# Clearing transfers one by one from the SP queue, and unread products of ones at four places, in a one-core transformer kernel

## The chip, the cores and the metric

The kernel runs on one core of one Trainium2 chip. The metric is device time in microseconds (us) of one execution, lower is better. TensorE (PE) multiplies, PEld loads its weights, VectorE (DVE), ScalarE (ACT) and GpSimd (POOL) do the elementwise work, and the queues of SP, ACT and POOL issue transfers (DMA).

## The reference

The input is one sequence of 512 tokens with 1024 features. The first block is differential attention and a mixture of 16 experts; the second has two layers (an even and an odd mixer, each followed by a gated feed-forward) and a last normalisation. The part around the change, cut to what matters:

```python
x = x + diff_attention(rmsnorm(x, norm_mix), ...)        # 8 heads, two softmaxes each
x = x + hier_moe(rmsnorm(x, norm_ffn), ...)              # 4 groups x 4 experts, 2 experts per token
for layer in range(2):
    h = h + (even_mixer if layer == 0 else odd_mixer)(rms_norm(h, ...), ...)
    h = h + conv_gated_ffn(rms_norm(h, ...), ...)
return rms_norm(h, norm_out_g)
```

In the expert part a token goes to the two best experts of its best group. Each expert has a gate and an up matrix (1024 x 512 each) and a down matrix (512 x 1024).

## The kernel before, in words

Activations lie with features on the 128 partitions (`h`, 8 chunks of 128 x 512). Every fp32 product is made from three matmuls: weights and activations are split into a rounded half and the rest (`wh`, `wl`; `xh`, `xl`), and `mm3` (L129 on, its matmuls are L135 to L141) adds three of the four cross products. ScalarE rounds the weights (`wh`, L110) and VectorE subtracts (`wl`, L111), so each stretch of matmuls needs both halves first.

The stages stand in the order of `run`: a (attention), b (experts), c (even mixer), d (feed-forward), e (odd mixer), f (feed-forward), z (last norm). `emit` runs a list of units of work, each with a cost in us, and `after(us, fn)` puts off a piece of work until units of that cost have gone by. A scheduler then orders the instructions of each engine before the run, so instructions that don't depend on each other can stand in another order than in the code. On the chip each engine takes its list strictly in order, and a waiting instruction holds all behind it.

Stage a. `project` makes q, k and v of four heads at a time. `headnorm` normalises q and k: ScalarE scales (`qs`, L449) and squares, VectorE sums and runs a reciprocal square root of 12 small steps (`rsq`, L286 to L293), VectorE scales (L466), TensorE transposes four 128 x 128 pieces (`t`, L472) into the one PSUM bank of that kind, and ScalarE copies them out (`kt`, two copies, L477). The next transposes wait for these copies. The first weights are split in four pieces of one chunk, as they land. `norm_r` takes the sums of squares through TensorE (`ss`, L349), then the same chain of small steps (`rt`).

After the first q and k, `moe_begin` loads constants, and `zero_rows` (L1254) clears the table `yb` in HBM, 1024 rows of 1024, to which the experts later scatter their results: one tile of zeros `zr`, 16 transfers of 256 KB, all issued by ScalarE's queue.

`route` (from L1298) makes the choice of experts: VectorE works out the logits and masks, TensorE counts ranks (`rk`, L1334) and finds the token numbers of the first two experts (`tk`, L1410), and POOL gathers the tokens' rows from HBM (`xe`, L1451). Stage b then starts: `weigh` (L1363) makes the weights `w` on VectorE and splits them on POOL into `tokv` (L1397), `places` picks them per expert (`tkb`, L1410), and `prep` transposes the gathered rows (L1462) and splits them (`xeh`, `xel`). `gate_up`, `act` and `down` run 16 experts. The last loop (L1600 on) adds the results into `h` and starts the next norm chunk by chunk; stage c begins with products of 290 columns.

`self.onesr` is a 128 x 128 tile of ones, `ptt` takes a PSUM bank of kind `t` (one in stage a, two in stage b).

Of the kernel before, what the change touches and what calls it, by code (L numbers as in the profile page):

```python
# [4 lines left out]
F32 = mybir.dt.float32  # L5
# [9 lines left out]
T, D, P = 512, 1024, 128  # L15
NT, NK = T // P, D // P
# [65 lines left out]
class K:  # L82
# [314 lines left out]
    def stage_a(self):  # L397
# [4 lines left out]
        with tc.tile_pool(name="pa", bufs=1) as pa:  # L402
# [6 lines left out]
            self.small_loads()  # L409
            dist = pa.tile([P, T], F32, name="c_dist")  # L410
            nc.sync.dma_start(dist, a["cst"][:, _CST["dist"][0]:_CST["dist"][0] + T])

            lv = pa.tile([P, 2, 64], F32, name="lv", tag="wk", bufs=6)
            ls = pa.tile([P, 2], F32, name="ls")
# [838 lines left out]

    def zero_rows(self, pool):  # L1254

        z = pool.tile([P, T], F32, name="zr", tag="wk", bufs=6)
        self.nc.gpsimd.memset(z, 0.0)
        for i in range(2 * NT):
            for c in range(2):
                self.nc.scalar.dma_start(self.yb[i * P:(i + 1) * P, c * T:(c + 1) * T], z)  # L1260

    def route_step(self, pool):

# [32 lines left out]
    def route(self):  # L1296
# [31 lines left out]
        Mb = pr.tile([P, NT, NE], BF, name="Mb")  # L1328
        nc.vector.tensor_tensor(Mb, f1, f2, op=OP.add)

        rk = self.pst("rk")
        for i in range(NT):
            for j in range(i + 1):
                nc.tensor.matmul(rk[:, i * NE:(i + 1) * NE], lhsT=self.onesb if j < i else self.before, rhs=Mb[:, j],  # L1334
                                 start=j == 0, stop=j == i, skip_group_check=True)
# [86 lines left out]
    def stage_b(self):  # L1422
# [5 lines left out]
        with tc.tile_pool(name="pb", bufs=1) as pb:  # L1428
# [20 lines left out]
            def gather(e):  # L1449
                xe = xes[e % 3]  # L1450
                nc.gpsimd.indirect_dma_start(out=xe, out_offset=None, in_=xn[:, :], bounds_check=T - 1, oob_is_err=False,  # L1451
                                             in_offset=bass.IndirectOffsetOnAxis(ap=self.gix[:, e:e + 1], axis=0))

            def prep(e):
                xe = xes[e % 3]
                xh = pb.tile([P, NK, P], F32R, name="xeh", tag="xeh", bufs=2)
                xl = pb.tile([P, NK, P], F32R, name="xel", tag="xel", bufs=2)
                for hf in range(2):
                    tp = self.ptt()
                    for q in range(4):  # L1460
                        kk = hf * 4 + q
                        nc.tensor.transpose(tp[:, q * P:(q + 1) * P], xe[:, kk * P:(kk + 1) * P], self.ident)  # L1462
                    sl = slice(hf * 4, hf * 4 + 4)
                    tv = tp.rearrange("p (a b) -> p a b", a=4)
                    nc.scalar.copy(xh[:, sl], tv)  # L1465
                    nc.vector.tensor_tensor(xl[:, sl], tv, xh[:, sl].bitcast(F32), op=OP.subtract)
                return xh, xl

            def gate_up(e, x):
                ps = []  # L1470
                for src in (wg[e], wu[e]):
                    acc = self.mmt()
                    sv = src.rearrange("(k p) n -> p k n", p=P)
                    for k0 in (0, 4):
                        raw = load(sv[:, k0:k0 + 4], 4, 512)
                        for c in (0, 2):
                            h, l = split(raw[:, c:c + 2], [P, 2, 512])
                            for k in (0, 1):
                                q = k0 + c + k
                                self.mm3(acc, h[:, k], l[:, k], x[0][:, q], x[1][:, q], q == 0, q == NK - 1, swap=True)  # L1480
                    ps.append(acc)
                return ps
# [63 lines left out]
            def spread(acc, e, y, m):  # L1546
                for n in range(2):
                    nc.tensor.matmul(acc, lhsT=y[n][:, m * P:(m + 1) * P], rhs=ohw[e], start=n == 0 and e == NE - 2, stop=False,
                                     skip_group_check=True)
# [12 lines left out]
            gather(0)  # L1562
            gather(1)
            self.weigh()
            tk = self.pvt("tkb")
            for e in range(2):
                self.places(e, tk, 6, 9)
            xs = {0: prep(0)}
            ps = gate_up(0, xs.pop(0))
            for e in range(2, 4):  # L1570
                self.places(e, tk, 0, 9)
# [2 lines left out]
            for e in range(NE - 2):  # L1574
# [5 lines left out]
                ps = gate_up(e + 1, xs.pop(e + 1))  # L1580
# [8 lines left out]
            ps = gate_up(NE - 1, xs.pop(NE - 1))  # L1589
# [9 lines left out]
            for m in range(NK):  # L1599
                acc = self.mmt()  # L1600
                spread(acc, NE - 2, yo, m)
                spread(acc, NE - 1, ye, m)
                for i in range(NT):
                    nc.tensor.matmul(acc[:, i * P:(i + 1) * P], lhsT=ys[i][1][:, m * P:(m + 1) * P], rhs=self.ident,
                                     start=False, stop=i == NT - 1, skip_group_check=True)
                self.last_add(m, acc)

    def overflow(self, pb):

# [224 lines left out]
```

## Time and profile before

| | |
|---|---|
| median of 3 runs | 1873.79 us (1873.08 to 1877.85) |
| the profiled execution | 1876.64 us, its span 1874.9 us |
| mean granted TensorE clock | 0.984 of full |
| PE, DVE, ACT, POOL busy | 97%, 69%, 54%, 12% of the span |
| HBM read, written | 238.19 MB, 15.73 MB |

The profile shows one execution. A busy PE need not be a fast one: a matmul of 512 columns starts every 0.23 us at the full clock and every 0.43 at the half clock, and the shares don't tell these apart. What ends the waits of each stretch, and how closely matmuls follow one another there, is read from the timelines.

### The profile page before, as it was taken

The numbers are of one execution on the slowest core, as the hardware profiler recorded it, in microseconds if no ns is written. First come the engines' busy times: TensorE is split into PE (matmuls) and PEld (weight loads), VectorE is DVE, ScalarE is ACT, GpSimd is POOL, SyncE is SP. The second block draws the span as 40 slices with busy tenths as digits, with TensorE's granted clock in tenths as the row PEclk, the third lists the DMA queues.
The fourth block names the chain that finished last, engine by engine and source line by source line (L and its number), as shares of the span: only waits on it lengthen the run. The fifth ranks groups of instructions, "written<-read, shape, count | busy, mean of one in ns | idle before, by whom it ended". The sixth has DMA issues, their size and how long they took to land.

```text
span 1874.9 us, 24863 instructions
## 1 busy us (share of the span) xinstructions
PE 1810.7 (97%) x8700; PEld 1464.2 (78%) x8701; DVE 1291.1 (69%) x2571; ACT 1019.8 (54%) x1787; POOL 222.5 (12%) x277
## 2 busy tenths in 40 slices
PE   8899997999998899999999999999999999999997
PEld 6688885778887787777888888888776788888885
DVE  6477857999997789755777357734567677537753
ACT  5467756888885347666544234433467544324442
POOL 2000012222222211320200000012100200000001
PEclk9899998999999899999999999999999999999998
DMA  5654657999995356562332333234544233243321
GB/s 193 206 136 116 177 166 267 353 370 368 371 368 188 108 138 167 135 164 74 107 98 69 104 108 106 69 97 135 145 127 108 75 91 100 77 121 91 91 85 61
DMA packets 278196, 287.36 MB, mean 153 GB/s; under 512 B 16150, under 2 KB 188598, under 8 KB 278064
## 3 DMA queue, kind: packets, MB, share of 16 engines
q1 hardware_dynamic: 268784, 270.15, 47.8%
q0 software_dynamic: 5072, 10.00, 1.5%
q10 hardware_dynamic: 4208, 5.56, 0.8%
q8 instruction: 70, 1.15, 0.3%
q14 instruction: 62, 0.51, 0.1%
HBM read 238.19 MB, written 15.73 MB: 135 GB/s over the span
## 4 chain that ended last, share of the span: by engine, by line
PE 59%; DVE 4%; DMA 1%; issue 1%; ACT 1%; POOL 1%; SPq 1%; DVEq 0%; POOLq 0%; ACTq 0%
PE mm L135 16%; PE mm L137 16%; PE mm L136 16%; PE pv L798 3%; PE s L765 2%; PE t L786 1%; DVE wl L111 1%; PE mm L140 1%; PE mm L139 1%; PE mm L141 1%; PE pv L1200 1%; DVE sc L964 1%; SPq L391 1%; DVE m L963 0%; DMA rsw<-qd 0%
## 5 line engine op out<-in xcount | busy, mean ns | idle before, releaser
L110 ACT CAST wh<-wr 128x1024 fp32r<-128x1024 f32 (+3 forms) x331 | 305.9, 925 | 361.9 <-PE mm L136 259.4
L111 DVE TENSOR_TENSOR wl<-wr,wh 128x1024 fp32r<-128x1024 f32 (+5 forms) x328 | 355.3, 1087 | 190.9 <-ACT wh L110 186.2
L135 PE MATMUL mm<-xh,wh 128*128 128x512 f32 x952 | 375.3, 394 | 2.1 <-DVE h L384 1.7
L137 PE MATMUL mm<-xh,wl 128*128 128x512 f32 x952 | 372.5, 391 | 0.0
L136 PE MATMUL mm<-xl,wh 128*128 128x512 f32 x952 | 371.9, 391 | 0.0
L135 PEld LDWEIGHTS mm<-xh,wh 128*128 128x128 f32 x952 | 179.2, 188 | 40.9 <-issue 4.2
L137 PEld LDWEIGHTS mm<-xh,wl 128*128 128x128 f32 x952 | 179.2, 188 | 38.2 <-issue 0.9
L136 PEld LDWEIGHTS mm<-xl,wh 128*128 128x128 f32 x952 | 179.3, 188 | 35.7
L111 DVE TENSOR_TENSOR wl<-wx,wh 128x1024 fp32r<-128x1024 f32 x123 | 151.9, 1251 | 13.0 <-ACT wh L110 6.8
L110 ACT CAST wh<-wx 128x1024 fp32r<-128x1024 f32 x134 | 139.5, 1050 | 25.2 <-PE mm L141 24.2
L139 PE MATMUL mm<-wh,xh 128*128 128x512 f32 (+3 forms) x384 | 138.1, 364 | 9.7 <-ACT wh L110 5.6
L140 PE MATMUL mm<-wl,xh 128*128 128x512 f32 (+3 forms) x384 | 137.5, 358 | 3.4 <-DVE wl L111 3.4
L137 PE MATMUL mm<-hh,wl 128*128 128x512 f32 x352 | 137.2, 390 | 0.0
L136 PE MATMUL mm<-hl,wh 128*128 128x512 f32 x352 | 137.1, 390 | 0.0
L135 PE MATMUL mm<-hh,wh 128*128 128x512 f32 x352 | 137.1, 389 | 0.0
L141 PE MATMUL mm<-wh,xl 128*128 128x512 f32 (+3 forms) x384 | 136.5, 356 | 0.0
L686 DVE TENSOR_TENSOR z<-mm,rb 128x512 f32<-128x512 f32 x88 | 60.3, 688 | 81.3 <-PE mm L137 81.3
L277 POOL TENSOR_TENSOR acc<-acc,sq 128x512 f32<-128x512 f32 x42 | 57.0, 1357 | 415.6 <-ACT sq L273 415.1
L139 PE MATMUL mm<-wh,xeh 128*128 128x512 f32 x256 | 103.6, 405 | 0.8 <-ACT xeh L1465 0.8
L140 PE MATMUL mm<-wl,xeh 128*128 128x512 f32 x256 | 101.6, 397 | 0.0
L141 PE MATMUL mm<-wh,xel 128*128 128x512 f32 x256 | 101.5, 396 | 0.0
L384 DVE TENSOR_TENSOR h<-mm,h 128x512 f32<-128x512 f32 x88 | 60.5, 689 | 47.1 <-PE mm L137 46.4
(414 smaller groups left out, 3394.9 us busy)
## 6 DMA issues: line engine op xcount, KB each, us to landing
wr<-in_ffn_w_up SPq DMA_DIRECT2D x88, 512.0 KB, 5.0
wx<-in_moe_w_gate SPq DMA_DIRECT2D x23, 1024.0 KB, 9.5
wx<-in_moe_w_up SPq DMA_DIRECT2D x22, 1024.0 KB, 8.9
wx<-in_moe_w_down SPq DMA_DIRECT2D x22, 1024.0 KB, 10.7
wr<-in_ffn_w_down SPq DMA_DIRECT2D x32, 704.0 KB, 4.7
kh<-nh SPq DMA_DIRECT2D x84, 128.0 KB, 2.3
wr<-in_moe_w_up SPq DMA_DIRECT2D x10, 1024.0 KB, 8.8
wr<-in_moe_w_down SPq DMA_DIRECT2D x10, 1024.0 KB, 11.3
```

What stands on the lines that cost most here:

```text
L110: nc.scalar.copy(h, raw)
L111: (nc.gpsimd if eng else nc.vector).tensor_tensor(l, raw, h.bitcast(F32), op=OP.subtract)
L135: mm(out, lhsT=wh, rhs=xh, start=first, stop=False, skip_group_check=True)
L136: mm(out, lhsT=wh, rhs=xl, start=False, stop=False, skip_group_check=True)
L137: mm(out, lhsT=wl, rhs=xh, start=False, stop=last, skip_group_check=True)
L139: mm(out, lhsT=xh, rhs=wh, start=first, stop=False, skip_group_check=True)
L140: mm(out, lhsT=xh, rhs=wl, start=False, stop=False, skip_group_check=True)
L141: mm(out, lhsT=xl, rhs=wh, start=False, stop=last, skip_group_check=True)
L277: nc.gpsimd.tensor_tensor(self.acc, self.acc, sq, op=OP.add)
L384: self.nc.vector.tensor_tensor(self.h[:, m], ps, self.h[:, m], op=OP.add)
L686: nc.vector.tensor_tensor(z[:, 2:], ps, self.rb, op=OP.mult)
L798: nc.tensor.matmul(pv[64 * e:64 * e + 64, j * P:], lhsT=heads[u]["v"](j), rhs=pt[:, 4 * j:3 * j + 4], start=j == 0, stop=j == NT - 1, skip ...
```

## The change

`zero_rows` makes the zeros in a tile of their own of 128 x 128, and issues 8 transfers of 512 KB (each partition's 512 bytes go out eight times) from SP instead of 16 of 256 KB from ScalarE, put off by 5, 11, ... 47 us of units. A new function `warm(n)` puts n matmuls of ones by ones (512 columns) into a bank of kind `t` that nobody reads; it is called at the start of stage a (6), before the rank counts of `route` (14), at the start of stage b (18) and after the last loop of stage b (8). In stage b `prep(0)` now stands ahead of the `places` of the first two experts.

```diff
--- before.py
+++ after.py
@@ -409,6 +409,7 @@
             self.small_loads()
             dist = pa.tile([P, T], F32, name="c_dist")
             nc.sync.dma_start(dist, a["cst"][:, _CST["dist"][0]:_CST["dist"][0] + T])
+            self.warm(6)
 
             lv = pa.tile([P, 2, 64], F32, name="lv", tag="wk", bufs=6)
             ls = pa.tile([P, 2], F32, name="ls")
@@ -1253,11 +1254,17 @@
 
     def zero_rows(self, pool):
 
-        z = pool.tile([P, T], F32, name="zr", tag="wk", bufs=6)
+        z = pool.tile([P, 128], F32, name="zr")
         self.nc.gpsimd.memset(z, 0.0)
         for i in range(2 * NT):
-            for c in range(2):
-                self.nc.scalar.dma_start(self.yb[i * P:(i + 1) * P, c * T:(c + 1) * T], z)
+            self.after(5 + 6 * i, lambda i=i: self.nc.sync.dma_start(
+                self.yb[i * P:(i + 1) * P].rearrange("p (c d) -> p c d", c=8), z[:, None, :].to_broadcast([P, 8, P])))
+
+    def warm(self, n):
+
+        ps = self.ptt("warm")
+        for _ in range(n):
+            self.nc.tensor.matmul(ps, lhsT=self.onesr, rhs=self.onesr[:, None, :].to_broadcast([P, NT, P]), start=True, stop=True)
 
     def route_step(self, pool):
 
@@ -1328,6 +1335,7 @@
         Mb = pr.tile([P, NT, NE], BF, name="Mb")
         nc.vector.tensor_tensor(Mb, f1, f2, op=OP.add)
 
+        self.warm(14)
         rk = self.pst("rk")
         for i in range(NT):
             for j in range(i + 1):
@@ -1562,10 +1570,11 @@
             gather(0)
             gather(1)
             self.weigh()
+            self.warm(18)
+            xs = {0: prep(0)}
             tk = self.pvt("tkb")
             for e in range(2):
                 self.places(e, tk, 6, 9)
-            xs = {0: prep(0)}
             ps = gate_up(0, xs.pop(0))
             for e in range(2, 4):
                 self.places(e, tk, 0, 9)
@@ -1604,6 +1613,7 @@
                     nc.tensor.matmul(acc[:, i * P:(i + 1) * P], lhsT=ys[i][1][:, m * P:(m + 1) * P], rhs=self.ident,
                                      start=False, stop=i == NT - 1, skip_group_check=True)
                 self.last_add(m, acc)
+            self.warm(8)
 
     def overflow(self, pb):
```

The changed lines move all numbers below them, by 1 after the first call, by up to 10 at the end. Three places of the engines' lists matter below.

ScalarE after the first q and k, before (`yb<-zr` are the clearing transfers, `kt` the copies out of the transposes' bank):

```order
L1246 DMA cr<-in_cst 128x388
L451 ACTIVATE sq<-qs 128x512
L1260 DMA yb<-zr 128x512 x16
L477 ACTIVATE kt<-t,vecs 128x2x128 x2
L110 CAST wh<-wr 128x1024 x2
L477 ACTIVATE kt<-t,vecs 128x2x128 x6
L716 CAST nh<-kt 128x512
L110 CAST wh<-wr 128x1024
```

and now:

```order
L1247 DMA cr<-in_cst 128x388
L452 ACTIVATE sq<-qs 128x512
L110 CAST wh<-wr 128x1024
L478 ACTIVATE kt<-t,vecs 128x2x128 x2
L110 CAST wh<-wr 128x1024
L478 ACTIVATE kt<-t,vecs 128x2x128 x6
L717 CAST nh<-kt 128x512
L110 CAST wh<-wr 128x1024
```

The 16 transfers are gone from the list, and one weight cast stands in their place. On SP the eight transfers now stand around the fifth of the first large weight loads; before it was

```order
L1717 DMA ident<-in_cst 128x128
L411 DMA c_dist<-in_cst 128x512
L128 DMA wr<-in_da_w_in 128x4x512 x5
L729 DMA qs<-nh 64x512
L730 DMA qs<-nl 64x512
```

and now

```order
L411 DMA c_dist<-in_cst 128x512
L128 DMA wr<-in_da_w_in 128x4x512 x4
L1260 DMA yb<-zr 1024x1x128 x5
L128 DMA wr<-in_da_w_in 128x4x512
L1260 DMA yb<-zr 1024x1x128 x3
L730 DMA qs<-nh 64x512
L731 DMA qs<-nl 64x512
```

VectorE at the end of the first four weight pieces, where the sums of squares `ss` come back from TensorE and `rtv` (L286) reads them; before:

```order
L311 SCALAR_TENSOR_TENSOR xl_110<-h,vecs,xh_108 128x512
L286 TENSOR_SCALAR rtv<-ss 128x4
L111 TENSOR_TENSOR wl<-wr,wh 128x1024
L287 TENSOR_SCALAR rty<-rtv 128x4
L111 TENSOR_TENSOR wl<-wr,wh 128x1024
L288 TENSOR_SCALAR rty<-rty 128x4
L291 TENSOR_TENSOR rtt<-rty 128x4
L292 SCALAR_TENSOR_TENSOR rtt<-rtt,rtv 128x4
```

and now:

```order
L287 TENSOR_SCALAR rty<-rtv 128x4
L288 TENSOR_SCALAR rty<-rty 128x4
L291 TENSOR_TENSOR rtt<-rty 128x4
L292 SCALAR_TENSOR_TENSOR rtt<-rtt,rtv 128x4
L293 SCALAR_TENSOR_TENSOR rt<-rtt,rty 128x4
L291 TENSOR_TENSOR rtt<-rt 128x4
L292 SCALAR_TENSOR_TENSOR rtt<-rtt,rtv 128x4
L293 SCALAR_TENSOR_TENSOR rt<-rtt,rt 128x4
L291 TENSOR_TENSOR rtt<-rt 128x4
L292 SCALAR_TENSOR_TENSOR rtt<-rtt,rtv 128x4
L293 SCALAR_TENSOR_TENSOR rt<-rtt,rt 128x4
L111 TENSOR_TENSOR wl<-wr,wh 128x1024 x3
```

The split of the next weights (`wl`, 128x1024) stood right behind the first small step, and stands now behind the whole chain; `rtv` is the row just ahead of the second list.

TensorE where the experts begin (`oh` are one-hot tiles, loaded as weights); before:

```order
L1410 MATMUL tk<-tokv,oh 128x6
L1462 MATMUL t<-ident,xe_3196 128x128 x8
L139 MATMUL mm<-wh,xeh 128x512
L140 MATMUL mm<-wl,xeh 128x512
L141 MATMUL mm<-wh,xel 128x512
L139 MATMUL mm<-wh,xeh 128x512
L140 MATMUL mm<-wl,xeh 128x512
L141 MATMUL mm<-wh,xel 128x512
L1410 LDWEIGHTS oh
L1410 MATMUL tkb<-tokv,oh 128x3
```

and now:

```order
L1418 MATMUL tk<-tokv,oh 128x6
L1267 MATMUL warm<-onesr 128x512 x18
L1470 MATMUL t<-ident,xe_3210 128x128 x8
L1418 LDWEIGHTS oh
L1418 MATMUL tkb<-tokv,oh 128x3
```

Three more `tkb` products follow, and then the expert products. The 18 products of ones stand ahead of the transposes of `prep(0)`, and the four `tkb` products, which read POOL's `tokv`, ahead of the first six expert products instead of behind them. On VectorE the last sum of `weigh` (`w`, L1388) stood behind the first `xel` of `prep(0)`, and stands now ahead of it. At the end of stage b the 8 products of the last call were parted: four stand behind the transposes of `hg` of the last expert, four behind the last loop.

## Rows read from the trace of the kernel before

**Rows 1.** The page, busy time: us, share of the span, instructions.
```profile
PE 1810.7 (97%) x8700; PEld 1464.2 (78%) x8701; DVE 1291.1 (69%) x2571; ACT 1019.8 (54%) x1787; POOL 222.5 (12%) x277
```

**Rows 2.** Timeline of ScalarE, 54 to 82 us: start, duration, instruction, [idle before, releaser].
```profile
61.26 10.38 ACTq L1260 DMA_DIRECT2D yb<-zr  x16
71.68 0.84 ACT L477 ACTIVATE kt<-t,vecs 128x256 f32<-128x256 f32 x2 [9.80 <-DMA yb<-zr]
```

**Rows 3.** Timeline of TensorE, 50 to 105 us; starts lie closer than durations, work overlaps.
```profile
61.46 0.39 PE L141 MATMUL mm<-wh,xl 128*128 128x512 f32 x1
...
64.41 0.60 PE L472 MATMUL t<-ident,qs 128*128 128x128 f32 x4
64.77 0.48 PE L139 MATMUL mm<-wh,xh 128*128 128x512 f32 x1
...
72.57 1.11 PE L472 MATMUL t<-ident,qs 128*128 128x128 f32 x4 [6.17 <-ACT kt L477]
...
79.53 0.60 PE L472 MATMUL t<-ident,qs 128*128 128x128 f32 x4
...
84.98 0.22 PE L526 MATMUL s<-kh,qs 128*128 128x128 f32 x1
```

**Rows 4.** Stretches: length, PE, PEld, DVE, ACT, POOL busy (count), PEclk, DMA share, GB/s.
```profile
5.60:10.40 4.80, 4.77 (x11) 3.46 (x12) 4.31 (x4) 4.41 (x8) 3.62 (x4) 1.00 1.04 391
...
30.00:40.00 10.00, 10.00 (x45) 8.26 (x45) 6.77 (x19) 7.12 (x10) 0.00 (x0) 1.00 0.01 3
...
280.00:281.00 1.00, 0.00 (x0) 0.00 (x0) 0.83 (x6) 0.58 (x1) 0.00 (x0) 0.62 1.05 403
```

**Rows 5.** Timeline of TensorE, 255 to 330 us.
```profile
279.32 0.64 PE L1288 MATMUL t<-ident,hg 128*128 128x128 f32 x4
285.00 0.17 PE L1334 MATMUL rk<-Mb,before 128*128 128x16 bf16 x1 [5.04 <-DVE Mb L1329]
...
293.35 1.94 PE L1462 MATMUL t<-ident,xe 128*128 128x128 f32 x8 [5.58 <-DMA xe<-xn,gix]
...
298.44 0.24 PE L1410 MATMUL tkb<-tokv,oh 128*128 128x3 bf16 x4 [0.67 <-POOL tokv L1397]
```

**Rows 6.** Timeline of TensorE, 574 to 665 us.
```profile
619.31 0.58 PE L139 MATMUL mm<-wh,xh 128*128 128x290 f32 x1 [3.18 <-DVE h L384]
...
625.28 0.30 PE L140 MATMUL mm<-wl,xh 128*128 128x290 f32 x1
...
627.42 0.30 PE L141 MATMUL mm<-wh,xl 128*128 128x290 f32 x1
```

**Rows 7.** Timeline of VectorE, 56 to 92 us.
```profile
67.28 1.29 DVE L466 TENSOR_TENSOR qs<-qs,rsq 128x512 f32<-128x512 f32 x2
```

**Rows 8.** Timeline of VectorE, 16 to 30 us.
```profile
22.95 1.23 DVE L111 TENSOR_TENSOR wl<-wr,wh 128x1024 fp32r<-128x1024 f32 x1
...
25.49 0.16 DVE L291 TENSOR_TENSOR rtt<-rty 128x4 f32<-128x4 f32 x1
...
27.06 0.16 DVE L293 SCALAR_TENSOR_TENSOR rt<-rtt,rt 128x4 f32<-128x4 f32 x1
```

**Rows 9.** Timeline of the SP queue, 0 to 120 us.
```profile
25.41 0.37 SPq L128 DMA_DIRECT2D wr<-in_da_w_in  x1
...
48.27 0.54 SPq L729 DMA_DIRECT2D qs<-nh  x1
```

**Rows 10.** The page, DMA issues: count, KB each, median us to landing.
```profile
wr<-in_ffn_w_up SPq DMA_DIRECT2D x88, 512.0 KB, 5.0
```

**Rows 11.** Timeline of TensorE, 20 to 33 us.
```profile
24.23 0.79 PE L140 MATMUL mm<-wl,xh 128*128 128x512 f32 x1 [0.35 <-DVE wl L111]
```

**Rows 12.** Timelines of ScalarE, VectorE and GpSimd, 276 to 312 us.
```profile
280.00 0.59 ACT L1290 COPY xk<-t 128x512 f32<-128x512 f32 x1 [1.20 <-PE t L1288]
...
295.09 0.69 DVE L1466 TENSOR_TENSOR xel<-t,xeh 128x512 fp32r<-128x512 f32 x1 [2.47 <-ACT xeh L1465]
...
295.98 0.47 POOL L1397 CAST tokv<-w 128x64 bf16<-128x64 f32 x1 [4.50 <-DVE w L1388]
```

## The prediction

> **What bounds the kernel now.** The page's busy times come first: TensorE has work in 97% of the span [rows 1], so a change counts by the gaps it closes in TensorE's row and by how fast the matmuls follow one another. I then looked for stretches with a gap and a low granted clock, and in each asked what ended the wait. Four matter here.
>
> First, ScalarE stands still for 10.38 us while it issues 16 clearing transfers, 0.65 us each [rows 2]. The copies `kt` behind them are needed by TensorE's next transposes, which wait 6.17 us and then run slowly [rows 3]. Second, at the start TensorE works at half clock: 11 matmuls take 4.8 us, 0.43 each [rows 4], against 0.23 at the full clock (13 from 61.46 to 64.41) [rows 3]; the clock column shows 1.00 there, so the spacing has to be read instead. Third, in the choice of experts TensorE waits for VectorE until 285.00 and for the gathered rows until 293.35 [rows 5], and its clock falls right at the first wait [rows 4]. Fourth, behind the experts it waits 3.18 us, and the products after that start slowly [rows 6].
>
> **The change, part by part.**
>
> *Clearing.* Without the issues on ScalarE, the transposes of 72.57 can start 6.17 us earlier. From there to the transposes of 79.53 TensorE took 6.96 us [rows 3] for four transposes twice and 13 matmuls. At the full clock that is twice 0.36 (64.77 less 64.41) [rows 3] and 13 x 0.23, 3.7 us, so 3.3 us more come back. Something is late next: VectorE's list now has a weight split inside the chain ahead of the scalings of 67.28 [rows 7]. A split of this size takes 1.23 [rows 8], so the scalings move to 68.5, and the first of the pair, half of 1.29, is ready at 69.15. The second transposes would start at 66.40 and end at 66.76, 7 matmuls bring TensorE to 68.37, and it waits 0.8. Sum: -6.2 - 3.3 + 0.8 = **-8.6 us**. The bounds are -9.4 (no new wait) and -6 (the clock falls all the same).
>
> The eight transfers cost SP eight issues, at ScalarE's 0.65 about 5 us. SP issues a load at 25.41 and has nothing that can't wait until 48.27 but one load [rows 9], and from 30 to 40 us the DMA share is 0.01 [rows 4]; five transfers fit there, three behind the next load. A load of the same size lands in 5.0 us [rows 10]. Cost: nothing. If that cover were gone, the weight loads and the stacked copies of q from 48.27 on would be late; the third rival prices this.
>
> The trace shows ScalarE held by the issues, with no wait of TensorE on the transfers' data [rows 2, 3]. The Trainium skill (DMA: Bandwidth & Descriptors, Issuing engines are not separate DMA queues) says that the engine which issues a transfer doesn't matter to the 16 DMA engines, and that another issuer saves only the issue time, usually small beside the transfer. By that rule the first term would be close to nothing and the sum -1.2; the trace bears out the first half of the rule, but here the issue is 10.38 us in front of waited-for work.
>
> *Six products at the start.* They need only the tile of ones and fill part of the wait until 5.63; six at 0.43 are 2.6 us, and the first real matmul isn't held up. What they can give is the slow start: 11 x (0.43 - 0.23) = 2.2 us at most [rows 3, 4], nothing at least. I take 1.7, since VectorE's list also has the third weight split earlier. But the list has moved something else: the next split stood right behind the first step on the sums, at 22.95, and now waits for 11 more small steps. Nine of these run from 25.49 to 27.06 [rows 8], 0.2 each, so it comes 2.2 us later. TensorE waited for just that split (0.35) at 24.23 [rows 11], so all of it shows. Together **+0.5**, bounds 0 and +2.2.
>
> *Fourteen and eighteen at the experts.* The 14 start when ScalarE has emptied the bank, at 280.59 (280.00 plus 0.59) [rows 12]. At full clock they last 3.2 us and are over at 283.8, before the ranks at 285.00; at half clock 6.0, until 286.6, and hold up the ranks, the token numbers and the gather by 1.6 [rows 5]. The clock fell between 280 and 281 (0.62 in that stretch) [rows 4], so I take half: +0.8. The 18 start at 287.77 (293.35 less 5.58): 4.1 us at full clock, done long before the gather lands; 7.7 at half, 2.1 too late. At the start the clock rose after some 4.8 us of slow matmuls; with 11 slow and 7 fast they end at 294.1. After that half the time they cost 0.7, so +0.4.
>
> Against this stands what the expert products gain. `tkb` now stands ahead of them and needs POOL's `tokv`, made from the last sum of the weights in 2.46 us (first step 295.98, product at 298.44) [rows 5, 12]. That sum stood behind a split for which VectorE waited from 292.62 to 295.09; now it stands ahead of the split, so it can run from 292.62 on, POOL starts some 0.2 later, and the small products come at 295.4. With 0.24 for them and 12 x 0.23, the twelfth expert product is over at 298.4. Before, the small ones came at 298.44, behind six expert products and a wait of 0.67, and six more, 1.4 us, ended at 300.1. That is -1.7. Place: +0.8 + 0.4 - 1.7 = **-0.5**, bounds -1.7 (full clock throughout) and +3.7 (1.6 + 2.1, nothing gained).
>
> *Eight behind the experts.* Four stand behind the last `hg` transposes and last 0.9 (4 x 0.23). They cost between nothing and that; ScalarE has to bring the transposes' results back before TensorE goes on, so I take 0.1. The other four shorten the wait of 3.18 to 2.3. From 619.31 to 625.28 came 25 products in 5.97 us; at the later pace (16 in 2.14, from 625.28 to 627.42 [rows 6]) they take 3.35. If the clock holds, 2.6 come back; it may still fall in 2.3 us of waiting, so I take half, 1.3. Together **-1.2**, bounds -2.6 and +0.9.
>
> Sum: -8.6 + 0.5 - 0.5 - 1.2 = -9.8 us. Against the profiled execution's own 1876.64 that is 1866.8. That execution lies 2.85 above the median of the runs, 1873.79, so the forecast for a median is **1864.0**, with -12 to -5 about it for the halves I took.
>
> **The rivals.**
>
> *The clock holds at every place.* No new wait behind the transposes (-9.4), nothing at the start, -1.7 at the experts, -2.6 behind them: -13.7, 1860.1. For it: each group stands where the clock fell. Against it: gaps are only shortened, and the clock fell at 280 almost with the last transposes.
>
> *The products of ones get in the way.* They are slow, because the clock falls before they start. +2.2 at the start, +3.7 at the experts, +0.9 behind them, against the -8.6: -1.8, 1872.0. For it: both waits at the experts end a chain through VectorE and POOL, so a delay of the ranks is paid in full.
>
> *SP is held by the clearing transfers* (slower). If each held the queue until it had landed, the copies of q of 48.27 would go out behind eight of them, at 25.8 + 8X. The first scores, which need them, come at 84.98 [rows 3]; 8.6 earlier that is 76.4, and less 5.0 for landing and the issues they may leave at about 70. So it decides from X = 5.5 us on. At 7.5 they leave at 85.8, 15.8 late, which gives -9.8 + 15.8 = +6 us, 1879.8. Against it: 16 issues on ScalarE took 0.65 each [rows 2], and 512 KB land in 5.0 [rows 10].
>
> *The gap stays.* Something else than the issues would hold the copies, or another wait takes all of its place. Then -1.2 is left, 1872.6. This is also what the rule above on issuing engines would give (the Trainium skill, same page). Against it: the copies follow within 0.1 us of the last issue [rows 2].
>
> **How the numbers follow.** Forecast 0.62, clock holds 0.18, in the way 0.12, gap stays 0.05, SP held 0.03. What a measurement can tell from no change is 0.3%, 5.6 us: below 1868.2 counts as faster, above 1879.4 as slower. The forecast's own spread falls short of this by 0.03 of its 0.62, the first rival never does, the second mostly (0.09 of 0.12), the gap that stays always. Faster 0.59 + 0.18 + 0.03 = 0.80; same 0.03 + 0.09 + 0.05 = 0.17; slower 0.03. The range reaches from just under the rival with the clock, 1858, to 1870, short of the one in the way: left out are most of that one, the two last ones, and a tail below.
>
> **What would show it.** ScalarE's row should have `kt` right behind the squares near 65 us, and no wait of TensorE above 1.5 us between 60 and 80. The eight transfers should be issued between 25 and 45 us at under 1 us each, no load late. VectorE should show the chain of small steps unbroken, with a wait of TensorE near 2.5 us behind it. At the experts the ranks would start at most 1.6 us later against the last transposes, and `tkb` ahead of the products. I am wrong if TensorE waits on SP's transfers before 100 us, or if the gain of the first 100 us isn't found again at 300: then something in between, the expert loads most likely, sets the pace.

## The result, and the profile after

| | before | after |
|---|---|---|
| median of 5 runs each | 1873.79 us (1872.66 to 1877.85) | 1863.22 us (1860.61 to 1866.81) |
| ratio of the runs, 95% interval | | 0.9945 [0.9934, 0.9956] |
| the profiled execution, its span | 1876.64, 1874.9 us | 1865.45, 1863.7 us |

The change saves 10.6 us of medians, 0.55%; forecast were 9.8. Where it comes from is read by following the same instruction of TensorE's list through both traces.

First the wait of the transposes [rows 2, 3]. Timelines of ScalarE, TensorE and VectorE after the change, 60 to 80 us:

```profile
65.88 0.84 ACT L478 ACTIVATE kt<-t,vecs 128x256 f32<-128x256 f32 x2 [2.23 <-PE t L473]
...
65.24 0.60 PE L473 MATMUL t<-ident,qs 128*128 128x128 f32 x4
...
67.06 0.60 PE L473 MATMUL t<-ident,qs 128*128 128x128 f32 x4
...
69.72 0.63 PE L473 MATMUL t<-ident,qs 128*128 128x128 f32 x4 [0.43 <-DVE qs L467]
...
76.82 0.22 PE L527 MATMUL s<-kh,qs 128*128 128x128 f32 x1
...
68.88 1.29 DVE L467 TENSOR_TENSOR qs<-qs,rsq 128x512 f32<-128x512 f32 x2
```

`kt` now follows its transposes (65.24) at once, and the next ones come at 67.06 with no wait; before, 72.57. The wait that replaces it is 0.43 us, for VectorE's scalings, which stand behind a weight split. From the 131st product (46.61) to the first scores (76.82) it is 30.21 us; before 39.18 (45.79, the line below, to 84.98 [rows 3]). The first scores come 8.2 us earlier, although the 131st product comes 0.8 later.

```profile
45.79 0.39 PE L140 MATMUL mm<-wl,xh 128*128 128x512 f32 x1
```

The timeline of the SP queue after the change:

```profile
26.59 10.22 SPq L1260 DMA_DIRECT2D yb<-zr  x5
...
40.24 0.37 SPq L128 DMA_DIRECT2D wr<-in_da_w_in  x1
40.65 6.17 SPq L1260 DMA_DIRECT2D yb<-zr  x3
49.08 0.52 SPq L730 DMA_DIRECT2D qs<-nh  x1
```

The clearing transfers by tile, in the changed kernel (duration of an issue in ns: least, middle, longest):

```profile
L1260 SPq DMA_DIRECT2D yb<-zr x8: 519/1386/5069, 26.6 to 41.9; - x8
```

and in the kernel before:

```profile
L1260 ACTq DMA_DIRECT2D yb<-zr x16: 336/645/842, 61.3 to 71.0; - x16
```

Eight issues took 16.4 us of SP's time (10.22 + 6.17), not 5, but the next load goes out at 40.24 and the copies of q at 49.08, 0.8 later than before [rows 9], as is all of TensorE's list by then.

Then the experts (TensorE; the last transposes of `hg`, the two groups of ones, the ranks, the transposes of the gathered rows, the 41st expert product), and the granted clock of four stretches there (columns as in rows 4):

```profile
271.29 1.09 PE L1295 MATMUL t<-ident,hg 128*128 128x128 f32 x4
273.06 5.62 PE L1267 MATMUL warm<-onesr 128*128 128x512 f32 x14 [0.68 <-ACT xk L1297]
278.53 0.18 PE L1342 MATMUL rk<-Mb,before 128*128 128x16 bf16 x1
...
281.95 7.14 PE L1267 MATMUL warm<-onesr 128*128 128x512 f32 x18 [0.68 <-DVE rs L1426]
288.93 1.04 PE L1470 MATMUL t<-ident,xe 128*128 128x128 f32 x8
...
300.07 0.39 PE L140 MATMUL mm<-wl,xeh 128*128 128x512 f32 x1
```

```profile
271.30:277.60 6.30, 5.62 (x16) 4.30 (x17) 5.56 (x32) 1.08 (x3) 2.75 (x6) 0.50 1.04 333
277.70:281.00 3.30, 2.08 (x25) 1.44 (x24) 1.93 (x15) 3.30 (x4) 0.01 (x1) 1.00 0.95 276
281.10:287.90 6.80, 6.12 (x17) 4.86 (x16) 4.06 (x18) 1.24 (x3) 5.47 (x7) 0.50 0.69 219
288.00:296.00 8.00, 7.83 (x44) 5.99 (x43) 5.17 (x14) 4.01 (x5) 0.00 (x0) 1.00 0.50 186
```

Both groups ran almost wholly at the half clock: 0.40 us for each product (5.62 / 14, 7.14 / 18). There is no wait left in front of the ranks nor of the gathered rows' transposes, because TensorE came to both late. From `hg` to the 41st expert product it took 28.78 us, against 27.38 before (279.32 [rows 5] to the line below).

```profile
306.71 0.39 PE L140 MATMUL mm<-wl,xeh 128*128 128x512 f32 x1
```

Behind the experts the wait is shorter, as forecast, and the clock of the products after it low for a shorter time:

```profile
608.11 1.05 PE L1613 MATMUL mm<-ident,ysum 128*128 128x128 f32 x8
608.92 1.18 PE L1267 MATMUL warm<-onesr 128*128 128x512 f32 x4
612.34 0.58 PE L139 MATMUL mm<-wh,xh 128*128 128x290 f32 x1 [2.24 <-DVE h L384]
...
619.23 0.29 PE L140 MATMUL mm<-wl,xh 128*128 128x290 f32 x1
```

The stretch of low clock there, before the change and after it (columns as in rows 4):

```profile
618.20:625.00 6.80, 5.69 (x23) 5.72 (x24) 3.93 (x4) 2.28 (x5) 5.12 (x8) 0.50 0.71 189
```

```profile
612.20:615.60 3.40, 3.26 (x13) 3.29 (x14) 2.96 (x2) 1.30 (x3) 3.38 (x5) 0.50 0.71 203
```

Followed along TensorE's list, the changed profile stands against the one before at +0.8 us at the 61st product, -8.2 at the first scores, -6.6 at the 41st expert product, -7.0 at the last product with `ysum`, -8.1 at the 41st product of 290 columns, and -10.9 at its end. The last 2.8 us are gained in a part that the change doesn't touch.

### The profile page after: what moved, and what is told of

The parts are those of the page before. It is cut to its first block, busy times and chain, and to the rows that moved or that the text cites. A ratio compares the mean times of both kernels' runs of the same rounds, so it can differ in the third digit from the quotient of the medians.

```text
span 1863.7 us, 24949 instructions
## 1 busy us (share of the span) xinstructions
PE 1820.4 (98%) x8746; PEld 1471.6 (79%) x8747; DVE 1288.4 (69%) x2571; ACT 1019.8 (55%) x1787; POOL 222.5 (12%) x277
## 4 chain that ended last, share of the span: by engine, by line
PE 60%; DVE 4%; DMA 1%; ACT 1%; POOL 1%; issue 1%; SPq 1%; DVEq 0%; POOLq 0%; ACTq 0%
PE mm L135 16%; PE mm L137 16%; PE mm L136 16%; PE pv L799 3%; PE s L766 2%; PE t L787 1%; PE mm L140 1%; PE mm L139 1%; PE mm L141 1%; PE pv L1201 1%; DVE wl L111 1%; DMA rsw<-qd 1%; DVE sc L965 1%; SPq L391 0%; DVE m L964 0%
## 6 DMA issues: line engine op xcount, KB each, us to landing
wx<-in_moe_w_down SPq DMA_DIRECT2D x22, 1024.0 KB, 10.9
wr<-in_moe_w_down SPq DMA_DIRECT2D x10, 1024.0 KB, 10.9
```

## The experiments

Twelve kernels. The times of a whole run scatter by some 5 us, so each row also gives five stretches of TensorE's own profiled list. **S**: start of the 61st product (`mm`, ones not counted). **K**: from the 131st to the first scores. **X**: from the last transposes of `hg` ahead of the ranks to the 41st expert product. **B**: from the last product with `ysum` to the 41st product of 290 columns. **E**: from there to the start of TensorE's last instruction. Ratios are to runs of the kernel before on the same chip, with their 95% interval.

| kernel | S | K | X | B | E | ratio, interval |
|---|---|---|---|---|---|---|
| before | 27.75 | 39.18 | 27.38 | 11.44 | 1237.8 | |
| before, again (e9) | 29.32 | 37.75 | 26.78 | 11.65 | 1237.6 | |
| changed | 28.58 | 30.21 | 28.78 | 10.34 | 1235.0 | 0.9945 [0.9934, 0.9956] |
| changed, again (e5) | 28.43 | 30.16 | 27.79 | 8.86 | 1233.8 | 0.9967 [0.9954, 0.9980] |
| e1, clearing alone | 26.27 | 30.18 | 27.00 | 10.31 | 1235.0 | 0.9961 [0.9948, 0.9974] |
| e2, ones alone | 28.34 | 37.98 | 27.66 | 10.43 | 1236.9 | 0.9998 [0.9989, 1.0008] |
| e3, without the 6 | 28.00 | 30.16 | 27.59 | 10.39 | 1234.7 | 0.9962 [0.9949, 0.9975] |
| e4, 9 and 12 | 28.52 | 30.17 | 25.22 | 10.31 | 1234.0 | 0.9960 [0.9947, 0.9973] |
| e6, without 14, 18 | 28.73 | 30.17 | 27.06 | 10.27 | 1235.0 | 0.9957 [0.9944, 0.9970] |
| e7, without the 8 | 28.48 | 30.20 | 28.91 | 10.34 | 1234.0 | 0.9954 [0.9941, 0.9967] |
| e8, 9 and 12 only | 29.41 | 30.18 | 25.38 | 10.41 | 1235.9 | 0.9952 [0.9940, 0.9964] |
| e10, 16 from SP | 27.72 | 32.58 | 26.76 | 10.33 | 1235.9 | 0.9962 [0.9946, 0.9977] |
| e11, 8 from ScalarE | 26.11 | 31.14 | 27.25 | 10.45 | 1238.5 | 0.9961 [0.9945, 0.9976] |
| e12, only 12 | 29.55 | 30.23 | 25.24 | 10.44 | 1236.6 | 0.9948 [0.9935, 0.9962] |

**e1, the clearing alone.** From the changed kernel all four calls of `warm` and the move of `prep(0)` are taken out:

```diff
-            self.warm(6)
-        self.warm(14)
-            self.warm(18)
-            xs = {0: prep(0)}
             tk = self.pvt("tkb")
...
+            xs = {0: prep(0)}
-            self.warm(8)
```

> The clearing on SP alone, without any product of ones and with prep(0) at its old place. Theory A (the 10.4 us of issues on ScalarE were the gain): TensorE's list runs level with the kernel before until 66 us, is 8.4 to 9.2 us ahead at 80 us, and keeps that through the experts, where nothing else is gained or lost: 1864.8 us, 1862 to 1867. Rival B (the products of ones keep the clock up and are the gain, the gap would have been filled by another wait): less than 3 us ahead at 80 us, 1871 to 1874.

Measured: 1863.43 us against 1872.33, and K falls to 30.18. The clearing alone gives the changed kernel's gain. Rival B falls. Theory A's "level until 66 us" misses: this profile was 1.5 us ahead at the 61st product already, and so 10.5 ahead at the first scores. The transposes that waited 6.17 us, in this kernel:

```profile
67.39 0.63 PE L472 MATMUL t<-ident,qs 128*128 128x128 f32 x4 [0.42 <-DVE qs L466]
```

**e2, the ones alone.** The changed kernel with `zero_rows` as it was before.

> The products of ones and the moved prep(0) alone; the zeros go out as before, 16 transfers from ScalarE. Theory A: the start 0.8 us late, the 6.2 us wait of the transposes back, 1.9 us lost at the experts, 1.3 gained behind them: 1.4 us slower than before, 1875.2, 1873 to 1877.5. Rival B (the ones are the gain): 4 to 5 us faster than before, 1868 to 1870.

Measured: 1872.72 against 1872.33, K 37.98. The wait is back:

```profile
73.84 1.11 PE L473 MATMUL t<-ident,qs 128*128 128x128 f32 x4 [6.11 <-ACT kt L478]
```

And the ones give nothing measurable. Theory A's 1.4 us slower isn't seen either, though the interval reaches that far; X is 27.66, so this profile lost less at the experts (0.3 us against the first profile of before, 0.9 against the second) than the 1.9 expected. Rival B falls.

**e3, without the six at the start.**

```diff
-            self.warm(6)
```

> The changed kernel without the six products at the start; VectorE's weight split then stands behind the first small step again, as it did before. Theory A (the six bring the first matmuls forward by 2.2 us, and the reordered split takes 3 back): level with the kernel before at 25 us instead of 0.8 late, 0.8 us better than the changed kernel, 1862.4. Rival B (the six pay for themselves, and the late split comes from another part of the change): the wait near 25 us is still there, 2.2 us slower than the changed kernel, 1865.4.

Measured: the wait near 25 us is 0.34 us instead of 1.90, as theory A has it, and the split is back in its place; S is 28.00, 0.6 less than in the changed kernel. It would be less still, but this execution waited 2.00 us for an earlier split, at 15.87, and the clock was low from 16.9 to 20.3. The total (0.9962) doesn't tell the theories apart. Over all profiles S is 28.34 to 28.73 in the six profiles with these products, and 26.11 to 29.55 in the eight without, mean 28.5 against 28.0. So the start is steadier with the six, and they cost half a microsecond, if anything.

**e4, 9 and 12 instead of 14 and 18.**

```diff
-        self.warm(14)
+        self.warm(9)
-            self.warm(18)
+            self.warm(12)
```

> The changed kernel with 9 instead of 14 and 12 instead of 18 products at the experts. Theory A (both groups ran at the half clock, 0.40 each, and were too long for their waits by 1.6 and 2.1 us): the ranks follow VectorE, 1.6 us earlier, the transposes of the gathered rows follow the DMA, 3.6 us earlier, and at most 2 us come back because the clock rises later among the expert products: 1.6 to 3.6 us better than the changed kernel, 1859.6 to 1861.6. Rival B (the gather and not the ones sets the transposes, and fewer ones lose the clock): the transposes no more than 1.6 us earlier, all of it given back by slow expert products, 1863 to 1866.

TensorE of this kernel, the same instructions as shown above:

```profile
272.05 0.63 PE L1295 MATMUL t<-ident,hg 128*128 128x128 f32 x4
273.35 2.33 PE L1267 MATMUL warm<-onesr 128*128 128x512 f32 x9 [0.68 <-ACT xk L1297]
277.72 0.17 PE L1342 MATMUL rk<-Mb,before 128*128 128x16 bf16 x1 [2.03 <-DVE Mb L1336]
...
281.13 4.81 PE L1267 MATMUL warm<-onesr 128*128 128x512 f32 x12 [0.68 <-DVE rs L1426]
285.78 1.03 PE L1470 MATMUL t<-ident,xe 128*128 128x128 f32 x8
...
297.27 0.39 PE L140 MATMUL mm<-wl,xeh 128*128 128x512 f32 x1
```

The ranks wait for VectorE again (2.03), 5.67 us behind `hg` instead of 7.24; the transposes of the gathered rows come 8.06 behind the ranks instead of 10.40. They still show no wait for the gathered rows, so the twelve end about when these land. X is 25.22, 3.6 less than in the first profile of the changed kernel, 2.6 less than in its second (e5), and 1.8 less than with no ones at all. The nine ran at the full clock here (2.33 us); in e8 the nine, and in e8 and e12 the twelve, ran at the half clock and X was the same, so this isn't what gains. In the total (0.9960) these us don't show: theory A holds for the place, and the total can't tell.

**e5, the changed kernel again, e6 without the 14 and the 18, e7 without the 8, e8 with 9 and 12 only** ran on one chip beside each other.

> The changed kernel as it is, beside the three below. Theory A (its gain is the clearing alone, 9.0 us, as in the run with the clearing alone; the ones lose about 1 at the start and 1 to 2 at the experts): 0.9950 of before, 1.5 to 3 us slower than the last kernel of this set. Rival B (the first ratio, 0.9945, was more than the clearing gave alone because the ones add 1 to 2 us): as fast as the last kernel or faster.

Measured: 1865.64 against 1871.50; 0.9967, where the first measurement gave 0.9945. The two intervals barely overlap: the change is worth 6 to 10 us, and is not known closer. e8 had 1863.87, 1.8 us faster in the median, as theory A has it, but the intervals overlap.

```diff
-        self.warm(14)
-            self.warm(18)
```

> The changed kernel without the 14 and the 18 products; the small tkb products then stand behind the first six expert products again. Theory A (the two groups hold up ranks and transposes by 3.7 us and give 2 us back in faster expert products): from the last transposes of hg ahead of the ranks to the 41st expert product 27.0 us, as before and with the clearing alone, against 28.8 in the changed kernel: about 1.5 us better than the changed kernel. Rival B (they pay): 30 us or more, slower than the changed kernel.

Its rows:

```profile
270.93 0.64 PE L1295 MATMUL t<-ident,hg 128*128 128x128 f32 x4
276.62 0.17 PE L1341 MATMUL rk<-Mb,before 128*128 128x16 bf16 x1 [5.05 <-DVE Mb L1336]
...
284.65 1.94 PE L1469 MATMUL t<-ident,xe 128*128 128x128 f32 x8 [5.26 <-DMA xe<-xn,gix]
286.41 0.80 PE L139 MATMUL mm<-wh,xeh 128*128 128x512 f32 x1
...
297.99 0.39 PE L140 MATMUL mm<-wl,xeh 128*128 128x512 f32 x1
```

X is 27.06, as forecast; without ones it is 26.76 to 27.38 in six profiles, with 14 and 18 it is 27.59 to 28.91 in five. This shows the two sides apart. Without ones the ranks come 5.69 behind `hg` and the transposes 8.02 behind the ranks; in the changed kernel 7.24 and 10.40: 1.6 and 2.4 us late. From the transposes to the 41st product it is 13.35 without and 11.14 with them: 2.2 us back, from a clock that is up (the eight transposes alone take 1.94 against 1.04) and from `tkb` being early. Net 1.7 lost. In e2, e3 and e5 one of the two groups ran in part at the full clock; there the delays of the ranks and of the transposes were 2.8 to 3.0 us in sum, against 3.9 in the changed kernel's first profile, and X (27.59 to 27.79) was still above the 27.04 that is the mean without ones.

```diff
-            self.warm(8)
```

> The changed kernel without the eight products behind the experts. Theory A (they gain nothing: the clearing alone, without them, also had the products behind the 3.2 us wait slow for only 3.4 us): from the last products with ysum to the 41st product of 290 columns 10.3 us, as in the changed kernel, and the same time within 0.1%. Rival B (they hold the clock, worth the 1.2 us of the prediction): 11.4 us there, as in the kernel before, 1.1 slower.

Its rows, to set beside those of the changed kernel:

```profile
608.05 1.05 PE L1613 MATMUL mm<-ident,ysum 128*128 128x128 f32 x8
612.28 0.58 PE L139 MATMUL mm<-wh,xh 128*128 128x290 f32 x1 [3.18 <-DVE h L384]
```

Measured: B 10.34, the same to the hundredth, with the whole 3.18 us wait back. The eight products gain nothing that this pair shows. Nor do four of them cost anything behind `hg`: from the 41st expert product to the last with `ysum` it is 308.8 us with them and 308.9 without. Rival B falls.

```diff
-            self.warm(6)
-        self.warm(14)
+        self.warm(9)
-            self.warm(18)
+            self.warm(12)
-            self.warm(8)
```

> The clearing, 9 and 12 products at the experts, none at the start and none behind the experts. Theory A: 0.3 to 1.5 us better at the start, 3.6 at the experts, nothing lost behind them: 3 to 5 us better than the changed kernel, 0.9935 of before or less. Rival B (the shorter groups did well in one profile only, by where the clock happened to fall): within 1.5 us of the changed kernel.

Measured: 0.9952, 1863.87. X is 25.38, as in e4, but S was 29.41, so the start took back what was hoped for there. It is 1.8 us better than the changed kernel in the median: between the two theories, and inside the scatter.

**e9, the kernel before again.**

> The kernel before, once more, for a second profile. Theory A (what the profile shown of before lost after the experts, 2.8 us from the 41st product of 290 columns to the end against every changed kernel, was that execution's own): 1234 to 1236 us there instead of 1237.8, and 39 us again from the 131st product to the first scores. Rival B (the change speeds up the later program): 1237 or more again.

Measured: K 37.75, the wait is there again; but E is 1237.6 again. Theory A's reading of the last 2.8 us misses. E lies between 1233.8 and 1238.5 among the twelve profiles with the change or part of it, so the low value isn't shown to belong to the change; it isn't explained as noise of one execution either. Where the 2.8 us go can be seen. Behind one wait of 2.15 us, the same in both kernels, the clock was low in the kernel before (columns as in rows 4):

```profile
652.40:655.70 3.30, 3.30 (x10) 2.62 (x9) 2.53 (x4) 1.48 (x3) 0.00 (x0) 0.50 0.23 43
```

and not in the changed one:

```profile
644.30:647.60 3.30, 3.30 (x17) 2.74 (x16) 2.58 (x4) 1.60 (x3) 0.00 (x0) 1.00 0.25 52
```

The changed list gains 1.6 us there. Another 1.1 it gains at a weight split that came late before, and that it didn't wait for:

```profile
787.25 0.40 PE L140 MATMUL mm<-wl,xh 128*128 128x290 f32 x1 [0.89 <-DVE wl L111]
```

The clock was low in the first of these places in five of the fourteen profiles, with and without the change (both of before, e2, e11, e12), and the wait of 0.8 to 0.9 us stood in the second in five (both of before, e3, e7, e11). What decides it stays open.

**e10, the 16 transfers at once, from SP.** In e1, `zero_rows` as before with one word changed:

```diff
-                self.nc.scalar.dma_start(self.yb[i * P:(i + 1) * P, c * T:(c + 1) * T], z)
+                self.nc.sync.dma_start(self.yb[i * P:(i + 1) * P, c * T:(c + 1) * T], z)
```

> No products of ones; the 16 transfers of 256 KB of the kernel before, all at once where they were, but issued by SP instead of ScalarE. Theory A (ScalarE's being held is the whole cost): 30 to 31 us from the 131st product to the first scores, as with the eight put off, against 39.2 before: 1863 to 1866. Rival B (spreading them out matters as much, because SP's loads and stacked copies behind them are then late by up to 10 us): 33 us or more, 1866 to 1872.

The SP queue, and TensorE's only wait for something between 50 and 100 us:

```profile
52.63 17.22 SPq L1260 DMA_DIRECT2D yb<-zr  x16
72.80 1.11 SPq L744 DMA_DIRECT2D kh<-nh  x2
...
69.15 0.63 PE L472 MATMUL t<-ident,qs 128*128 128x128 f32 x4 [0.54 <-DVE qs L466]
```

K is 32.58, between the two; but TensorE doesn't wait for it. The scores stand some products later in its list, and at 102 us it is 1.7 us behind e1, where it was 1.6 behind at 27 us. The row's 17.22 us hold 8.5 of issues; in the rest SP waited for two earlier transfers, and the stacked copies behind them still came in time. Theory A holds, though its figure for K doesn't.

**e11, the eight put-off transfers from ScalarE.** In e1:

```diff
-            self.after(5 + 6 * i, lambda i=i: self.nc.sync.dma_start(
+            self.after(5 + 6 * i, lambda i=i: self.nc.scalar.dma_start(
```

> No products of ones; the eight put-off transfers of 512 KB, issued by ScalarE instead of SP. Theory A (an issue holds the engine that issues it, on SP 1.1 us in the middle and up to 4.7, and ScalarE has waited-for casts behind each): 5 to 10 us lost again somewhere before 65 us, 1868 to 1874. Rival B (the rule that the issuer doesn't matter much, and only the bunch of 16 did): within 2 us of the clearing from SP, 1862 to 1866.

ScalarE and its queue:

```profile
20.88 7.47 ACTq L1259 DMA_DIRECT2D yb<-zr  x3
...
29.04 1.05 ACT L110 CAST wh<-wr 128x1024 fp32r<-128x1024 f32 x1 [7.63 <-PE mm L141]
...
63.44 0.84 ACT L477 ACTIVATE kt<-t,vecs 128x256 f32<-128x256 f32 x2 [2.23 <-PE t L472]
```

Three issues in a row took 7.47 us of ScalarE, and cost nothing: the cast behind them waited for TensorE anyway (7.63). K is 31.14, but the 131st product stands elsewhere in this list, and at the first scores TensorE is 0.1 us ahead of e1, as it was near 27 us; the ratio is that of e1. Theory A falls. It isn't that ScalarE issues; it is that 16 issues stood right in front of the copies that TensorE needed next.

**e12, only the 12.** e8 without the nine.

> The clearing and 12 products ahead of the gathered rows' transposes, no other products of ones. Theory A (the 12 alone do the work of both groups; the others give nothing): 25.2 to 25.6 us from the last transposes of hg to the 41st expert product, as with 9 and 12, and 0.9935 to 0.9955 of before. Rival B (without the group ahead of the ranks the clock comes back too late): 26.5 us or more.

Measured: X 25.24, 0.9948. The 12 alone do it.

## Why the prediction was right, and where it was not

**Clearing, -8.6: right.** Measured -9.0 (K, 39.18 to 30.21), and shown by e1 and e2 to come from this part alone. Against the second profile of the kernel before it is -7.5: behind the same wait the clock was low for 6.8 us there, and for 10.3 in the first. The new wait was 0.43 instead of 0.8, and the clock held from 60 to 80 us (granted 1.00). The rule on issuing engines (the Trainium skill, DMA: Bandwidth & Descriptors, Issuing engines are not separate DMA queues) was weighed as a rival with the gap kept. It says that all transfers share the same 16 DMA engines whoever issues them, and that another issuer saves only the issue time, usually small. The trace of before alone could not show the first half; e10 agrees with it, where the same 16 transfers landed in 3.1 us in the middle from SP, against 3.0 from ScalarE. The second half leaves out what stands behind the issues: the one word changed in e10 took 10.38 us [rows 2] from in front of the copies, and with them the wait of 6.17 us and its slow clock.

**SP's eight issues, "Cost: nothing": right, for the reason given, with a wrong size.** They took 16.4 us, not 5, and not under 1 us each. The cover held it, and e10 shows that even 17 us of SP some 26 us later hide.

**The start, +0.5: right in the sum, by luck.** +0.8 in the profile, 0.5 in the means, from two sizes that were both too small. The gain, taken as 1.7, was 2.7 by the 46th product (17.59 against 20.30): 1.4 from faster early products, most of the rest from two waits for earlier splits that grew shorter. The loss, taken as 2.2, was 3.5 from there to the 61st. The wait for the split that stands behind the chain was 1.90, as meant:

```profile
25.03 0.80 PE L140 MATMUL mm<-wl,xh 128*128 128x512 f32 x1 [1.90 <-DVE wl L111]
```

But TensorE also waited 0.86 us for ScalarE's squares ahead of it (20.40), and the clock was low for 6.8 us from 21.7 on, where before it was low for 3.4 from 24.3.

**The experts, -0.5: wrong, +1.4 in the profile.** The step that failed is "I take half": both groups ran at the half clock, so the ranks came 1.6 us late and the transposes 2.4, where 0.8 and 0.4 were taken. These are about the upper bounds that the prediction gave (1.6 and 2.1). Where one group ran in part at the full clock (e2, e3, e5), the two delays were still 2.8 to 3.0 us in sum, where 1.2 was taken. The gain was sized at -1.7 and measured -2.2 (e6). The rival that the ones get in the way described this place; it was held for 0.12.

**Behind the experts, -1.2: the number came true (-1.1), its cause did not.** Without the eight products B is as short (e1, e7, e8). The clock was low for 6.8 us in both profiles of the kernel before, for 3.4 in all others but one, and in one of the changed kernel (e5) not at all. What decides this isn't settled; the step that took half of what a held clock gives, on account of the eight products, is not borne out. The Trainium skill (TensorE: Matmul & The Clock Gate, Part 1) says that how many matmuls run slow changes from run to run of one kernel, by where the clock's monitor stands when it starts. The two profiles of the changed kernel, 10.34 and 8.86 there, agree that it changes from run to run; no run here shows the reason.

**The sum.** -9.8 against -10.6 measured first and -5.9 in the second measurement. That it met the first so well is partly luck: the experts gave 1.9 us less than forecast, and 2.8 came from the untouched part E.

## What to carry to other kernels

Look for long runs of DMA issues on a compute engine's queue, and ask what stands behind them: moving them to another engine or to another time was worth the same here (e10, e11), and a slow issue is free where its engine waits anyway. Count products that keep TensorE busy in a wait at the half clock, and let them end about when the wait does: against the mean without ones, 14 and 18 lost 0.6 to 1.9 us of X where 12 gained 1.8, and the same idea at two other places gave nothing that could be measured. When parts of a change are worth 1 to 3 us and a run scatters by 5, read the stretches of the profile and not the totals.

## What was not expected

An issue can hold its engine for long: the eight transfers of 512 KB took 0.52 to 5.07 us each on SP in the changed kernel, and the 16 of 256 KB 0.34 to 0.84 on ScalarE. And products added on TensorE can change VectorE's list: the six at the start moved a weight split behind 11 small steps there, with 1.90 us of waiting for it, and what the early clock gave (2.7 us) was lost again by the 61st product.
